# TensorE's order in two stages of a two-block transformer kernel: steps tied to the order in which the program records them

## The chip, the cores and the metric

One core of a Trainium2 chip runs the whole program. The metric is the device time of one execution in microseconds (µs). The engines are TensorE (PE, matrix products; its weight loads are shown as PEld), VectorE (DVE), ScalarE (ACT), GpSimd (POOL) and SyncE (SP), whose queue issues the transfers. Each engine takes the instructions of its own queue in the order that was fixed when the program was compiled.

## What is computed

The reference is two transformer blocks over 1024 tokens of width 1024, in float32. Block 1 projects the normalized input to seven parts and mixes them in two ways. The parts q, f and i feed HGRN, a linear recurrence with a gate per channel, over 4 heads of width 128:

```python
S_new = jnp.exp(b_last[:, :, 0, :])[..., None] * S + jnp.einsum(
    'bhsk,bhsv->bhkv', kb * jnp.exp(b_last - b), vb)
return S_new, o_inter + o_intra
```

The parts sq, sk and sv feed stick-breaking attention, strictly causal, over 8 heads of width 64:

```python
rem = lax.cumsum(log_1mb, axis=3, reverse=True) - log_1mb
a = jnp.where(causal, jnp.exp(jax.nn.log_sigmoid(z) + rem), 0.0)
outs.append(jnp.einsum('bhts,bshd->bthd', a.astype(v.dtype), vp))
```

Both results are normalized (the HGRN one is also gated by hg), joined and multiplied by w_out. A gated feed-forward and an embedding gate follow, and then block 2, with two other kinds of attention, a feed-forward with a convolution, and a gate.

## The kernel before, in words

Every projection is done in three matmuls (mm3, lines 300 to 302): weights and activations are split into a high and a low part, and high by high, high by low and low by high are added in one PSUM bank. A weight unit is 128 x 1024 numbers. Its life is: a load (line 110) into one of two raw buffers; a cast to the high part on ScalarE (line 218); a subtraction for the low part on VectorE or GpSimd (line 224); its matmuls; then its buffer, one of four, is free for the next unit. All transfers are issued from SyncE's queue.

**Steps.** The two stages in question are written as lists of steps. A step is a pair of a cost in assumed µs and a function that records the step's instructions on all engines. A projection step is six matmuls of 512 columns (a_steps and b_steps: a group of 24 matmuls in four steps of 5.1 / 4 = 1.275 each); the fourth step of a group also records what empties the bank, and lets the next weight units be split (pump).

**HGRN stage** (mix1, hgrn_steps). Head 0's own projections (16 steps) and the first two HGRN steps of head 0 are recorded one after the other (run). Then merge interleaves two lists. The first holds the other HGRN steps. Each head has 12: diag (cost 1.7; line 732), seven levels for n = 1, 2, 4, ... 64 (1.7 each; line 746), kt (0.9; transposes, line 779), ds (1.7; line 796) and two outputs (1.7 each; lines 818 and 820). A level multiplies the running q and k products on TensorE, then VectorE multiplies half of q (line 763) and GpSimd half of k (line 764) by the products of gates, and the next level needs both. The second list holds 112 projection steps: head 1's q and f, the first half of pair 0 for the other attention, head 2's q and f, the second half of pair 0, head 3's q and f, sv in 32 steps, and pair 1.

**Stick-breaking stage** (sb, attention_steps, pv_steps). The first list has 236 attention steps with a sum of costs of 119.28, the second the 64 projection steps that mix1 returns (pairs 2 and 3, and the gate hg), with a sum of 81.6. For a head and a block of 128 rows, score multiplies q by k (lines 968, 969; line 971 adds the mask), ScalarE takes two sigmoids (lines 972, 973), VectorE runs a scan along the row (line 975) and a product (line 977). For two blocks of rows and two of columns, one step transposes (line 869), ScalarE and VectorE split the result (lines 872, 873), and a later step multiplies it by the values (lines 882, 886, 888) in the stage's one bank for values; when a pair of row blocks is through, ScalarE copies half of that bank (line 892) and VectorE adds it up (line 983). After two heads, after_pair transposes the pair's result (line 992), takes squares (line 996) and stores it (line 999). Transposes have two banks, scores three, projections two; the split operand has two buffers.

**What sets the order.** merge takes from its first list while that list's share of its cost is at most by times the share of the second list. That is the order in which instructions are recorded. The compiled order is another thing: the tile framework's scheduler goes through the program with its own timing, and gives each engine, whenever it is free, the ready instruction with the lowest priority number. The number is the place of recording; around a step of the first list, merge lowers it by ahead, which is 0 for the HGRN stage and 300 for the stick-breaking stage (AHEAD). So where a step is not ready in the scheduler's timing, the engine's queue gets a later one first.

**After the two stages** out1 multiplies the two results by w_out: for each 128 tokens, prep loads the HGRN output, its gate and the attention output and transposes the gated HGRN output (line 288); mm does two groups of matmuls for each half of the columns, the first on the HGRN part, the second on the attention part. Its weight units take the buffers that the hg units leave.

Of the kernel before, what the change touches and what calls it, by code (L numbers as in the profile page):

```python
# [43 lines left out]
AHEAD = dict(hg=0, sb=300, mla=-20, diff=100)  # L44
BY = dict(hg=1.05, sb=1.0, mla=0.75, diff=1.0)
# [151 lines left out]
class Kernel:  # L197
# [125 lines left out]
        self.u = [self.up.tile([P, 2, 8, 512], F32R, tag="u", name=f"u{h}") for h in range(2)]  # L323


    def merge(self, main, side, ahead=0, by=1.0):


        tc = self.tc
        tm, tsd = sum(c[0] for c in main) or 1, sum(c[0] for c in side) or 1  # L330
        i = j = 0
        a = b = 0.0
        while i < len(main) or j < len(side):
            one = j >= len(side) or (i < len(main) and a / tm <= by * b / tsd and (len(main[i]) < 3 or j >= main[i][2]))
            f = (main[i] if one else side[j])[1]
            if one:
                a, i = a + main[i][0], i + 1
                tc.cur_priority -= ahead
                f()
                tc.cur_priority += ahead  # L340
            else:
                b, j = b + side[j][0], j + 1
                f()


    def a_units(self, name, c0, n):
# [296 lines left out]
    def mix1(self):  # L643
        nc, S, U = self.nc, self.S, self.U
        st = nc.sync.dma_start
        with ExitStack() as c:
            vp = self.pool("hg_v", 1, ctx=c)
            tmp = self.htmp = self.tmp
            v = vp.tile([P, NT, 512], F32, name="hg_vt")
            self.hg_v = v  # L650
            self.first(v)
            self.constants_late()
            self.hp = self.pool("hg", 2, ctx=c)
            self.h1p = self.pool("hg1", 1, ctx=c)
            H = [dict() for _ in range(4)]

            def ev_q(h):
                def f(ps, half):
                    if half == 0:
                        H[h]["q"] = self.hp.tile([P, T], F32, tag="q", name="hq")  # L660
                    s = tmp.tile([P, 512], F32, tag="s", name="sg")
                    nc.scalar.activation(s, ps, AF.Sigmoid)
                    nc.vector.tensor_tensor(H[h]["q"][:, half * 512:(half + 1) * 512], ps, s, ALU.mult)
                return f

            def ev_f(h):
                def f(ps, half):
                    if half == 0:
                        H[h]["f"] = self.hp.tile([P, T], F32, tag="f", name="hf", bufs=1)
                        H[h]["k"] = self.hp.tile([P, T], F32, tag="k", name="hk")  # L670
                    c = slice(half * 512, (half + 1) * 512)
                    lb, mlb = self.lb[:, 0, h:h + 1], self.lb[:, 1, h:h + 1]
                    s = tmp.tile([P, 512], F32, tag="s", name="sg")
                    nc.scalar.activation(s, ps, AF.Sigmoid)
                    nc.vector.tensor_scalar(H[h]["f"][:, c], s, mlb, lb, op0=ALU.mult, op1=ALU.add)
                    s = tmp.tile([P, 512], F32, tag="s", name="sg")
                    nc.scalar.activation(s, ps, AF.Sigmoid, scale=-1.0)
                    nc.vector.tensor_scalar(H[h]["k"][:, c], s, mlb, None, op0=ALU.mult)
                return f

            def ev_T(dst, j):
                def f(ps, half):
                    t = tmp.tile([P, 2, 512], F32R, tag="hl", name="stage")
                    self.split(t[:, 0, :], t[:, 1, :], ps, "act", "dve")
                    c = slice(half * 512, (half + 1) * 512)
                    for e in range(2):
                        st(out=dst[2 * j + e, :, c].rearrange("(a r) t -> r a t", a=2), in_=t[e * 64:(e + 1) * 64].bitcast(F32))
                return f

            def ev_sv(ps, i):  # L690
                t = tmp.tile([P, 8, 2, 64], F32R, tag="hl", name="stage")
                self.split(t[:, :, 0, :], t[:, :, 1, :], ps.rearrange("p (h d) -> p h d", h=8), "act", "dve")
                st(out=S["sv"][i * P:(i + 1) * P], in_=t.rearrange("p h a d -> p h (a d)").bitcast(F32))

            def ev_gate(ps, i):
                s = tmp.tile([P, 512], F32, tag="s", name="sg")
                nc.scalar.activation(s, ps, AF.Sigmoid)
                nc.vector.tensor_tensor(s, ps, s, ALU.mult)
                st(out=S["hgg"][i * P:(i + 1) * P, :], in_=s)

            def head(h):
                return self.a_steps(U["hq", h][0], ev_q(h)) + self.a_steps(U["hf", h][0], ev_f(h))

            def pair(j):
                return (self.a_steps(U["sq", j][0], ev_T(S["sq"], j))
                        + self.a_steps(U["sk", j][0], ev_T(S["sk"], j)))

            first = head(0)
            p0 = pair(0)
            main = head(1) + p0[:8] + head(2) + p0[8:] + head(3) + self.b_steps(U["sv"], self.u_of, ev_sv) + pair(1)  # L710
            side = []
            for h in range(4):
                side += self.hgrn_steps(h, H[h])
            self.run(first + side[0:2])
            self.merge(side[2:], main, AHEAD["hg"], BY["hg"])
        return pair(2) + pair(3) + self.b_steps(U["hg"], self.u_of, ev_gate)

    def hgrn_steps(self, h, X):
# [220 lines left out]
    def sb(self, rest):  # L939
        nc, S, U, A = self.nc, self.S, self.U, self.A  # L940
        self.banks = {"d": [0, 1], "z": [2, 3, 4], "tr": [5, 6], "pv": [7]}
        with ExitStack() as c:
# [56 lines left out]
                nc.sync.dma_start(out=S["osbT"][j * P:(j + 1) * P, :], in_=o)  # L999

            side = self.attention_steps(8, load, score, make_put, after_pair, ORDER["sb"], lambda h: max(0, h // 2 - 1) * 16)
            self.merge(side, rest, AHEAD["sb"], BY["sb"])


    def out1(self):
# [4 lines left out]
        with ExitStack() as c:  # L1010
# [15 lines left out]
            def prep(i):  # L1026
                o = ip.tile([P, 512], F32, tag="o", name="o_hg")
                ld(out=o, in_=S["ohg"][i * P:(i + 1) * P, :])
                gt = ip.tile([P, 512], F32, tag="gt", name="gate")
                ld(out=gt, in_=S["hgg"][i * P:(i + 1) * P, :])  # L1030
                sb = ip.tile([P, 4, P], F32, tag="sb", name="o_sb")
                ld(out=sb, in_=S["osbT"][:, i * P:(i + 1) * P].rearrange("(k p) t -> p k t", p=P))
                r = self.rstd_sqrt(self.square_sum(o, 512), 512)
                nc.gpsimd.tensor_tensor(gt, o, gt, ALU.mult)
                nc.vector.scalar_tensor_tensor(out=o, in0=gt, scalar=r, in1=g_hg, op0=ALU.mult, op1=ALU.mult)
                OT[i] = u = op.tile([P, 2, 8, P], F32R, tag="oT", name="oT")
                self.split(u[:, 0, 4:8, :], u[:, 1, 4:8, :], sb, "act", "gps")
                return lambda: self.transpose_split(o, u, 0, 0, 4)
# [937 lines left out]
```

## Time and profile before

| | |
|---|---|
| Median of 3 executions | 2896.67 µs (2895.93 to 2899.95) |
| The profiled execution | 2897.28 µs, span 2895.5 µs |
| TensorE busy, share of the span | 2777.6 µs, 96% |
| VectorE busy | 1756.3 µs, 61% |
| ScalarE busy | 1163.4 µs, 40% |
| GpSimd busy | 712.3 µs, 25% |
| Mean granted TensorE clock | 0.991 of full speed |

The span runs from the first instruction's start to the last one's end; the execution's time has 1.8 µs more around it. Times of rows are µs from the span's start. In the rows, PE is TensorE, SPq the queue of SyncE; "bank" is a PSUM bank, hk and hg_qp are the running k and q products of HGRN, be and om the rows of the attention, at the transposed ones. Matmuls are pipelined and their ends are modelled, so the durations of neighbours overlap: what a matmul costs is the time from its start to the next one's. Idle time in brackets is that of the engine just before the row, with what ended it.

### The profile page before, as it was taken

To read this page: it belongs to the slowest core of one execution; us is meant where nothing else is said; L and a number is where in the kernel's file an instruction comes from. 1 tells how busy PE (TensorE), PEld (TensorE's weight loads), DVE (VectorE), ACT (ScalarE), POOL (GpSimd) and SP (SyncE) were. 2 spreads that over 40 slices of the span, in tenths; PEclk is the share of its full clock that TensorE was granted. 3 is DMA by queue.
4 is the path that set the end of the run, shared out by engine and by line. 5 is a ranking of instruction groups with operands and counts; after the bars stand their busy time and mean duration, and the time that the engine had idled before them with its cause. 6 is when DMAs were issued, how large, how long until landed. Compare 5 with 4: busy or idle time off the path is not lost. (4 is left out here: it accounts for less than half of the span.)

```text
span 2895.5 us, 37271 instructions
## 1 busy us (share of the span) xinstructions
PE 2777.6 (96%) x13699; PEld 2281.7 (79%) x13699; DVE 1756.3 (61%) x3132; ACT 1163.4 (40%) x2237; POOL 712.3 (25%) x608
## 2 busy tenths in 40 slices
PE   8989998988999999999999999989999999999999
PEld 6878767776888888887788788767778888788887
DVE  4444598768444334667478775777875555556661
ACT  4211376745333334223246455656543333311131
POOL 1222100035433332223124000020243343222211
PEclk9989999999999999999999999999999999999999
DMA  4221645252322224332126855753422222343211
GB/s 134 73 71 65 175 124 135 93 183 73 95 87 84 83 78 165 102 104 91 65 102 178 217 151 175 203 131 76 139 73 81 80 88 87 118 166 104 77 65 46
DMA packets 277942, 321.36 MB, mean 111 GB/s; under 512 B 14646, under 2 KB 207194, under 8 KB 276222
## 3 DMA queue, kind: packets, MB, share of 16 engines
q1 hardware_dynamic: 277758, 318.97, 36.5%
q8 instruction: 108, 1.77, 0.3%
q14 instruction: 76, 0.62, 0.1%
HBM read 228.69 MB, written 92.59 MB: 111 GB/s over the span
## 5 line engine op out<-in xcount | busy, mean ns | idle before, releaser
L1249 PE MATMUL bank<-q,w 128*128 128x512 f32 x3696 | 846.6, 391 | 5.9 <-DVE q L1132 1.4
L1249 PEld LDWEIGHTS bank<-q,w 128*128 128x128 f32 x3696 | 693.3, 188 | 157.6 <-ACT s L1186 2.1
L218 ACT CAST w<-raw 128x1024 fp32r<-128x1024 f32 (+2 forms) x246 | 236.8, 971 | 495.9 <-DVE y L1315 185.9
L224 DVE TENSOR_TENSOR w<-raw,w 128x1024 fp32r<-128x1024 f32 (+2 forms) x242 | 311.7, 1297 | 128.1 <-ACT w L218 121.7
L1315 DVE TENSOR_TENSOR y<-y,bank 128x512 f32<-128x512 f32 x336 | 227.0, 686 | 162.1 <-PE bank L302 158.3
L300 PE MATMUL bank<-w,act 128*128 128x512 f32 x704 | 274.7, 390 | 2.7 <-DVE o L1231 2.7
L302 PE MATMUL bank<-w,act 128*128 128x512 f32 x704 | 274.7, 391 | 1.5 <-POOL act L224 1.5
L300 PE MATMUL bank<-w,u 128*128 128x512 f32 (+1 forms) x672 | 272.0, 405 | 3.1 <-DVE dn L1574 1.4
L301 PE MATMUL bank<-w,act 128*128 128x512 f32 x704 | 274.5, 390 | 0.0
L301 PE MATMUL bank<-w,u 128*128 128x512 f32 (+1 forms) x672 | 266.4, 396 | 3.3 <-POOL w L224 2.2
L302 PE MATMUL bank<-w,u 128*128 128x512 f32 (+1 forms) x672 | 265.9, 396 | 1.1 <-DVE u L296 1.1
L224 POOL TENSOR_TENSOR act<-act_raw,act 128x1024 fp32r<-128x1024 f32 x40 | 103.6, 2609 | 300.9 <-ACT act L218 300.9
L1186 ACT COPY s<-bank 128x512 f32<-128x512 f32 x132 | 77.4, 588 | 202.6 <-PE bank L1249 202.5
L300 PEld LDWEIGHTS bank<-w,act 128*128 128x128 f32 x704 | 132.6, 188 | 30.7 <-DVE o L1231 3.1
L302 PEld LDWEIGHTS bank<-w,act 128*128 128x128 f32 x704 | 132.5, 188 | 30.0 <-POOL act L224 2.2
L301 PEld LDWEIGHTS bank<-w,act 128*128 128x128 f32 x704 | 132.4, 188 | 27.2
L300 PEld LDWEIGHTS bank<-w,u 128*128 128x128 f32 x672 | 127.3, 189 | 26.6 <-ACT u L293 2.4
L301 PEld LDWEIGHTS bank<-w,u 128*128 128x128 f32 x672 | 127.2, 189 | 26.8 <-POOL w L224 3.1
L302 PEld LDWEIGHTS bank<-w,u 128*128 128x128 f32 x672 | 127.0, 189 | 26.2 <-DVE u L296 1.7
L224 DVE TENSOR_TENSOR w<-s,w 128x1024 fp32r<-128x1024 f32 x44 | 54.4, 1236 | 139.9 <-ACT w L218 139.9
L873 DVE TENSOR_TENSOR at<-bank,at 128x512 fp32r<-128x512 f32 (+1 forms) x160 | 99.8, 630 | 42.8 <-ACT at L872 41.6
L140 POOL TENSOR_TENSOR s<-raw 128x512 f32<-128x512 f32 x44 | 59.9, 1362 | 218.3 <-DVE w L224 137.4
(361 smaller groups left out, 5208.9 us busy)
## 6 DMA issues: line engine op xcount, KB each, us to landing
raw<-in_w_gate_up_dram SPq DMA_DIRECT2D x44, 512.0 KB
act<-o SPq DMA_DIRECT2D x88, 256.0 KB
raw<-in_w_down_dram SPq DMA_DIRECT2D x44, 512.0 KB
act_raw<-act SPq DMA_DIRECT2D x44, 512.0 KB
raw<-in_w_in_dram SPq DMA_DIRECT2D x40, 512.0 KB
qk<-qkT SPq DMA_DIRECT2D x32, 384.0 KB
raw<-in_w_gate_dram SPq DMA_DIRECT2D x22, 512.0 KB
raw<-in_w_up_dram SPq DMA_DIRECT2D x22, 512.0 KB
```

The costliest lines, as they stand in the source:

```text
L140: pool(x[:, HI], r2[:, LO], r2[:, HI], ALU.add)
L218: nc.scalar.copy(hi, src)
L224: e.tensor_tensor(lo, src, hi.bitcast(F32), ALU.subtract)
L300: mm(ps, lh, rh, start=start, stop=False)
L301: mm(ps, lh, rl, start=False, stop=False)
L302: mm(ps, ll, rh, start=False, stop=stop)
L873: nc.vector.tensor_tensor(at[:, 1, 0:w], ps[:, 0:w], at[:, 0, 0:w].bitcast(F32), ALU.subtract)
L1186: nc.scalar.copy(t, src)
L1249: nc.tensor.matmul(ps, w[:, a, o], (uh, ul)[b][:, k, :], start=bool(first) and n_mm == 0, stop=n_mm == 11, skip_group_check=True)
L1315: nc.vector.tensor_tensor(y, y, ps, ALU.add)
```

## The change

merge gets a parameter, fixed. With it, each step is recorded inside tc.issue_after(last), where last is the TensorE instruction that was recorded last before the step. This call of the tile framework gives every instruction that the step records on TensorE an edge to last: it is placed behind it in TensorE's queue, and does not wait for its end. So no TensorE instruction of a step can be placed ahead of the step before it. Other engines get no edge, and neither do instructions outside the two calls. The HGRN and the stick-breaking stage use it; two other calls of merge stay as they are.

```diff
-    def merge(self, main, side, ahead=0, by=1.0):
+    def merge(self, main, side, ahead=0, by=1.0, fixed=False):
         tc = self.tc
+        traced = self.nc.cur_bb.bb.instructions
+
+        def step(f):
+            last = next((x for x in reversed(traced) if x.engine == self.nc.tensor.engine), None) if fixed else None
+            with tc.issue_after(last) if last is not None else ExitStack():
+                f()
+
...
                 a, i = a + main[i][0], i + 1
                 tc.cur_priority -= ahead
-                f()
+                step(f)
                 tc.cur_priority += ahead
             else:
                 b, j = b + side[j][0], j + 1
-                f()
+                step(f)
...
-            self.merge(side[2:], main, AHEAD["hg"], BY["hg"])
+            self.merge(side[2:], main, AHEAD["hg"], BY["hg"], fixed=True)
...
-            self.merge(side, rest, AHEAD["sb"], BY["sb"])
+            self.merge(side, rest, AHEAD["sb"], BY["sb"], fixed=True)
```

## Rows read from the trace of the kernel before

**Rows 1.** The page: busy µs of each engine, share of the span, instructions.

```profile
PE 2777.6 (96%) x13699; PEld 2281.7 (79%) x13699; DVE 1756.3 (61%) x3132; ACT 1163.4 (40%) x2237; POOL 712.3 (25%) x608
```

**Rows 2.** Stretches (µs): length, then busy and count of each engine, PEclk, DMA.

```profile
90.62:113.64 23.02, 21.04 (x129) 17.34 (x128) 13.73 (x15) 2.62 (x4) 9.91 (x11) 1.00 0.30 106
...
163.90:169.90 6.00, 3.51 (x32) 3.40 (x32) 2.16 (x3) 0.00 (x0) 1.09 (x1) 1.00 0.00 0
169.90:187.00 17.10, 10.75 (x61) 10.05 (x60) 4.93 (x10) 4.14 (x6) 5.75 (x3) 0.50 0.00 1
...
338.65:565.18 226.53, 206.20 (x1227) 162.49 (x1226) 199.52 (x259) 152.76 (x379) 5.95 (x60) 1.00 0.43 116
565.18:577.69 12.51, 12.51 (x59) 10.33 (x58) 5.98 (x16) 11.44 (x27) 3.11 (x2) 1.00 0.85 289
577.69:620.00 42.31, 33.60 (x138) 25.79 (x136) 27.42 (x47) 19.35 (x36) 16.37 (x10) 0.93 0.65 213
```

**Rows 3.** TensorE's timeline, head 0's front: start, µs, line, shapes, [idle before].

```profile
91.43 0.48 PE L300 MATMUL bank<-u,w 128*128 128x512 f32 x1
...
96.35 1.99 PE L746 MATMUL bank<-hg_qp,hk 128*127 128x64 f32 x16 [0.34 <-DVE hg_qp L727]
...
99.61 0.40 PE L301 MATMUL bank<-u,w 128*128 128x512 f32 x1
100.65 1.94 PE L746 MATMUL bank<-hg_qp,hk 128*126 128x64 f32 x16 [0.64 <-DVE hg_qp L763]
...
104.75 1.92 PE L746 MATMUL bank<-hg_qp,hk 128*124 128x64 f32 x16 [0.49 <-DVE hg_qp L763]
...
108.66 1.86 PE L746 MATMUL bank<-hg_qp,hk 128*120 128x64 f32 x16 [0.33 <-DVE hg_qp L763]
```

**Rows 4.** TensorE's timeline, three of head 1's steps.

```profile
164.46 1.86 PE L746 MATMUL bank<-hg_qp,hk 128*120 128x64 f32 x16 [0.56 <-DVE hg_qp L763]
168.25 1.76 PE L746 MATMUL bank<-hg_qp,hk 128*112 128x64 f32 x16 [1.93 <-DVE hg_qp L763]
172.32 2.83 PE L746 MATMUL bank<-hg_qp,hk 128*96 128x64 f32 x16 [2.31 <-POOL hk L764]
```

**Rows 5.** ScalarE's timeline around head 1's copies and the two weight casts.

```profile
179.44 0.58 ACT L750 COPY hg_sc<-bank 64x512 f32<-64x512 f32 x1 [32.98 <-PE bank L746]
...
183.64 1.99 ACT L218 CAST w<-raw 128x1024 fp32r<-128x1024 f32 x2
```

**Rows 6.** SyncE's queue: the bias transfer and the weight loads behind it.

```profile
78.96 0.73 SPq L572 DMA_DIRECT2D skew<-bias  x1
82.77 18.24 SPq L110 DMA_DIRECT2D raw<-in_w_in_dram  x2
```

**Rows 7.** VectorE in 340 to 566, by line and shape: count, busy µs, mean ns, idle before.

```profile
L873 DVE TENSOR_TENSOR at<-bank,at 128x512 fp32r<-128x512 f32 x48 | 32.4, 679 | 3.1 <-ACT at L872 2.9
L975 DVE TENSOR_TENSOR_SCAN om<-om,zeros 128x1024 f32<-128x1024 f32 x8 | 18.3, 2282 | 0.5 <-ACT om L972 0.4
...
L983 DVE TENSOR_TENSOR sb_o<-bank,ot 64x256 f32<-64x256 f32 x32 | 13.1, 411 | 2.4 <-ACT ot L892 1.9
...
L977 DVE TENSOR_TENSOR be<-be,om 128x1024 f32<-128x1024 f32 x8 | 9.7, 1215 | 0.1
```

**Rows 8.** ScalarE in 340 to 566, the same view.

```profile
L872 ACT CAST at<-bank 128x512 fp32r<-128x512 f32 x48 | 28.2, 593 | 21.0 <-PE bank L869 20.5
...
L973 ACT ACTIVATE be<-bank 128x512 f32<-128x512 f32 x40 | 24.1, 603 | 0.0
...
L892 ACT COPY ot<-bank 64x256 f32<-64x256 f32 x32 | 11.8, 370 | 9.9 <-PE bank L888 9.4
...
L996 ACT ACTIVATE junk<-bank 128x128 bf16<-128x128 f32 x28 | 8.1, 289 | 1.2 <-PE bank L992 1.0
```

**Rows 9.** TensorE's waits in 338 to 566: total µs, times, longest.

```profile
PE bank L882 <- DVE sb_o L983: 10.0, 16, 1.2
```

**Rows 10.** TensorE's timeline, the first matmul of the output stage.

```profile
580.37 0.50 PE L300 MATMUL bank<-w,oT 128*128 128x512 f32 x1 [2.24 <-ACT oT L293]
```

## The prediction

> **What bounds the kernel now.** The page comes first: TensorE is busy for 96% of the span [rows 1], so time is won or lost only where TensorE waits or runs slowly. The change touches two stages, so the second view is the table of stretches [rows 2]. Read there the share of TensorE and its granted clock. Head 0's front of the HGRN stage (90.62 to 113.64) loses 2.0 µs of idle time. From 163.90 to 187.00, in head 1, TensorE is busy for 14.3 of 23.1 µs, and for 17.1 of them the granted clock is 0.50, which is 1.2 GHz. The stick-breaking stage (338.65 to 565.18) leaves 20.3 µs idle while VectorE is busy for 199.5 of 226.5 µs. Behind it stand 54 projection matmuls alone: 12.5 µs with no idle time, 0.23 µs a matmul, and VectorE is busy there for only 6.0 µs.
>
> The third view is the program's order. In merge the HGRN steps that are left sum to 75.0 (4 heads of 19.6, less two steps of 1.7) and the projection steps to 112 × 1.275 = 142.8. A level of 1.7 is 2.27% of its list, a projection step 0.89%; with by = 1.05 some 2.4 steps of six matmuls, 14 matmuls or 3.3 µs, follow each level. I counted the matmuls of lines 300 to 302 ahead of each HGRN step in the trace against these sums. They agree within two (records can be missing) from level 16 of head 0 to level 4 of head 1 (336 to 474) and from head 2's first step to the end (594 to 918). **They differ in two places**: head 0's front, and head 1 from level 8 to its outputs, which all stand behind 480 matmuls where the program has 486 to 582. Only there does the tie move TensorE in this stage.
>
> **The change, part by part.** It adds no instruction. It takes from the scheduler the choice of what TensorE does next at a step's border; VectorE, ScalarE, GpSimd and the DMA queue are placed anew around that order.
>
> **Head 1 of HGRN: −14.0.** Idle time is 2.49 + 6.35 = 8.84 µs [rows 2]: each level waits for the VectorE or GpSimd product of the level before, with no filler between [rows 4]. The 10.75 busy µs of the slow stretch take 5.4 at 2.4 GHz, so 5.3 more; together 14.2, less some 0.2 for a short wait such as other heads have. The tie puts 12 to 18 matmuls (2.8 to 4.1 µs) between levels. A level needs 4.3 µs from start to start, 2.0 of it TensorE's own (from 96.35 to 100.65 in [rows 3]), so 2.3 µs of cover are enough.
>
> Why there was no filler matters, since the tie could put TensorE before the same obstacle. The next projection step was that of head 2's forget gate. Its two weight casts ran on ScalarE at 183.64, after ScalarE had idled for 33 µs, and behind head 1's copies in its queue [rows 5]; their loads had been issued by 101 [rows 6]. So the place in the queue was late, not the data. A 2.4 MB bias transfer was issued just ahead of those loads, at 78.96 [rows 6]; I read the order as one made by a scheduler that expected them late. Under the tie the cast must stand ahead of head 1's level 8 on ScalarE, or the program could not end, and there it finds an idle engine. What stays is its VectorE half (1.2 µs), likely placed behind level 4's products: **+1.0**, bounded by 0 and by 3 (a sigmoid, the cast and the VectorE half one after the other, 0.6 + 1.05 + 1.2).
>
> **Head 0's front: +3.8.** The first two steps are recorded before the merge, and every projection step of the merge stands behind level 2. The 20 matmuls that now fill the gaps up to 100.65 (from 91.43 to 99.61, 20 of them) [rows 3] move behind it: 20 × 0.23 = 4.6 µs. Level 2 comes no earlier, since each step there already ended a wait for VectorE. Behind it the program has 18 and 12 matmuls where the trace has 7 and 7, so the waits of 0.49 and 0.33 at 104.75 and 108.66 go: 4.6 − 0.8 = 3.8.
>
> **The clock at that front: +1.0**, between 0 and 5. The row nearest to it is head 1's, where gaps of 0.56 and 1.93 µs preceded the fall to 0.50 [rows 2, 4]; the new front has gaps of about 1.8, 1.8 and 2.3 in 10 µs, but then 18 matmuls without one. If the fall comes, two levels cost 1 µs more each, and a part of the 18 matmuls (4.1 µs) doubles. I take 1.0 as the middle of no fall and a short one.
>
> The Trainium skill (TensorE: Matmul & The Clock Gate, "HAM oscillation — how this bites in real kernels") says that waits between groups of matmuls throw the clock back to its lower level, so that the work behind starts slowly; by that rule this term would be an estimated 4 to 5 µs and the total some 3 to 4 µs longer. The trace agrees where gaps come in a row (0.50 from 169.9 to 187.0), and disagrees for single ones: the stick-breaking stage keeps 1.00 with 20 µs of gaps.
>
> **The stick-breaking stage and its hand-over: −3.0.** Gains and losses nearly balance here. Now attention steps are pulled ahead by a priority of 300, and the projections lag until 54 are left over (12.5 µs). Tied, 64 projection steps lie evenly between 236 attention steps, so these 54 become filler. But TensorE can no longer go round a wait. To size the new waits I walked all steps in the program's order with start-to-start intervals of this trace (transposes 0.109, 256-column matmuls 0.118, 512-column ones 0.235 µs), each other engine taking what is ready, attention first. TensorE's work is 195.6 µs: 90.2 of projections, 31.4 of transposes, 34.1 of values, 36.4 of scores, 3.5 at the pairs' ends. The waits sum to 42.2:
> - transposes behind the rows they need, 14.8: sigmoid 0.60, scan 2.28, product 1.22 [rows 7, 8] are 4.1 µs, against some 3 µs of steps between; 7.7 of the 14.8 fall on head 0, where no older work is queued;
> - values behind their split operand, 11.7: 0.59 + 0.68 µs, plus a scan that happens to be running;
> - values behind the add that frees the only bank, 10.4: 0.37 + 0.41 and three hops make 0.9; today's idle from this cause is 10.0 [rows 9];
> - steps behind the four squares of a bank at a pair's end, 5.3 [rows 8].
>
> 195.6 + 42.2 = 238. The same walk over today's order, taken from the trace, ends at 244.7 where the trace has 241.1 (the last gate's product): it runs 1.5% long. Other choices of VectorE's and ScalarE's order moved the tied walk between 237 and 246. On the trace's scale, projections end some 6 µs earlier than 577.69, but attention ends some 8 µs later than 565.4. The output stage needs both: its weights follow the projections' end, its second operand the last pair's store. Today its first group starts at 580.37 after 2.24 idle [rows 10] and its second half near 583. Tied, the first half can start near 576 and the second near 580. That is −3.0, bounded by −9 (all waits behind 580 vanish as well) and by +9 (the walk's upper end, and nothing won at the hand-over).
>
> **Sum:** −14.0 + 1.0 + 3.8 + 1.0 − 3.0 = −11.2. The profiled execution took 2897.28 µs (span 2895.5 and 1.8 around it), 0.6 above the median of 2896.67. 2897.3 − 11.2 = 2886.1: I forecast **2886**.
>
> **The rivals.**
> *Late weights take the gain back.* If the cast of head 2's gate still stands behind something late on ScalarE or VectorE, TensorE stops at that step rather than in the levels, and the queue of head 1 stops behind it. For it: two casts, a sigmoid and a store all stood late together. Against: in the tied order little is left that the cast can stand behind, and ScalarE idled for 33 µs [rows 5]. Price: 8 to 12 of the 14 µs come back; 2896.
>
> *The tied attention waits more than the walk says: slower.* VectorE is 88% busy in that stage [rows 2], and each of the 80 transposed groups makes a round trip through ScalarE and VectorE to which TensorE is now tied. The walk has 42.2 / 80 = 0.53 µs of wait a group. At 0.75, a quarter of a mean scan more, the stage loses 18: 2904. It decides from 0.14 µs a group (11.2 / 80) on. For it: the order's spacing counts steps by assumed costs, not by VectorE's time. Against: the walk stayed below 246 for every order of the other engines.
>
> *The tie does nothing*, as priorities give the order anyway: so it is for most of three HGRN heads, but not in the stretches that carry the sum.
>
> **How the numbers follow.** Forecast 0.62, late weights 0.20, tied waits 0.15, no effect 0.03. A measurement of this kernel can tell about 0.2%, 5.8 µs, from no change. Faster is the forecast's 0.62, same the 0.23 of late weights and no effect, slower 0.15. The forecast alone reaches from 2874 (no half clock, −9 at the attention) to 2891; late weights carry the range to 2897, and the lower part of the slower case to 2901.
>
> **What would show it.** After the change head 1's levels should stand 12 to 18 matmuls apart with the clock at 1.00; the two casts should run on ScalarE before head 1's level 8; head 0's first four HGRN steps should stand with no projection between; no run of 54 projections should follow the attention; TensorE's idle time should rise in the attention, mostly ahead of lines 869 and 882, to about 40 µs. It is wrong if idle time there passes 55 µs, or if TensorE waits over 5 µs at head 2's gate.

## The result and the profile after

The changed kernel takes **2925.9 µs** (median) against 2896.3 for the kernel before in the same comparison: a ratio of 1.0105, 95% interval 1.0093 to 1.0117. It is slower by some 30 µs where 11 µs less were forecast, and outside the range. The profiled execution has a span of 2924.3, 28.8 more than before.

Where the 28.8 went, by the start or end of the same instructions in the two traces:

| from, to | before | after | difference | predicted |
|---|---|---|---|---|
| head 0's first scores to head 1's (HGRN) | 55.1 | 63.4 | +8.3 | +4.8 |
| head 1 to head 2 | 70.1 | 58.3 | −11.8 | −13 |
| head 2 to the first score of the attention | 124.8 | 125.6 | +0.8 | 0 |
| first score to the end of attention and projections | 237.1 | 265.5 | **+28.3** | with the next row, −3 |
| to the first matmul of the stage behind the output stage (line 1126, now 1134) | 47.9 | 53.2 | **+5.3** | |
| from there to the end of the span | 2269.9 | 2267.8 | −2.1 | 0 |

The HGRN stage did what was forecast, with a dearer front: the first score stands at 337.93 instead of 340.57. The stick-breaking stage and its hand-over lost 33.6.

The table of stretches of the kernel after, in the columns that [rows 2] have (length; busy µs of each engine with counts; granted clock of TensorE; share of the DMA engines; GB/s):

```profile
90.72:115.00 24.28, 18.50 (x90) 16.53 (x89) 10.87 (x12) 2.02 (x3) 8.76 (x10) 0.72 0.29 102
...
154.07:212.34 58.27, 56.38 (x343) 48.60 (x342) 29.92 (x38) 13.63 (x20) 12.55 (x14) 1.00 0.30 85
336.10:603.20 267.10, 224.38 (x1279) 181.85 (x1277) 207.70 (x266) 159.94 (x387) 5.95 (x60) 0.96 0.39 106
603.20:614.13 10.93, 0.19 (x3) 0.03 (x1) 5.28 (x16) 8.06 (x23) 1.26 (x1) 0.56 0.94 311
95.92:109.57 13.65, 10.85 (x41) 9.93 (x42) 5.12 (x6) 0.00 (x0) 4.08 (x6) 0.50 0.32 112
409.94:416.77 6.83, 5.57 (x19) 4.50 (x18) 1.25 (x2) 2.70 (x10) 0.00 (x0) 0.50 0.16 65
604.50:624.98 20.48, 7.90 (x22) 6.14 (x23) 11.05 (x24) 10.80 (x28) 6.25 (x5) 0.50 0.90 305
```

Head 1 now runs at clock 1.00 with 1.9 µs of idle time. Head 0's front fell to 0.50 for 13.65 µs. The attention stage is 267.1 long with 42.7 idle; before, its two stretches in [rows 2] were 239.0 with 20.3 idle. Of the stage's 28.1, 22.4 are therefore idle time. The clock makes most of the rest: 409.94 is one of five stretches at 0.50, 20.5 µs together, in which TensorE is busy for 19.2; half of that, 9.6, is what the lower level costs. The two sum to 32.0, 3.9 more than the stage lost. In the walk's counting that remainder is waiting which the modelled ends show as busy: of the 239.0 before, 195.6 are the walk's work and 20.3 idle, which leaves 23.1; the same difference after, 267.1 − 195.6 − 42.7 − 9.6, is 19.2.

TensorE's waits of the kernel after from 336 to 604 (engine and line, releaser, total µs, times, longest), which answer to [rows 9]:

```profile
PE bank L890 <- DVE sb_o L991: 12.3, 16, 1.3
PE bank L877 <- ACT junk L1004: 10.2, 6, 2.1
PE bank L877 <- DVE be L985: 9.3, 13, 2.0
PE bank L890 <- DVE at L881: 8.8, 11, 1.5
```

All line numbers of the two stages stand 8 higher than before: 890 is the values' matmul, 877 the transposes, 991 the add that frees the bank, 1004 the squares at a pair's end. The second line is new; the third was 2.0 before and the fourth 5.0.

How such a wait arises is seen at the first pair's end, in TensorE's and then ScalarE's timeline of the kernel after (start, µs, operation; idle time and releaser in brackets):

```profile
406.41 1.04 PE L1000 MATMUL bank<-ident,sb_o 128*128 128x128 f32 x8
409.57 0.58 PE L877 MATMUL bank<-ident,be 128*128 128x128 f32 x3 [2.12 <-ACT junk L1004]
411.40 1.12 PE L877 MATMUL bank<-ident,be 128*128 128x128 f32 x4 [1.26 <-ACT junk L1004]
```

```profile
407.72 1.14 ACT L1006 ACTIVATE sb_o<-sb_o,cols 128x1024 f32<-128x1024 f32 x1
...
411.16 0.19 ACT L1004 ACTIVATION_READ_ACCUMULATOR junk<-bank 128x1 f32 x1
```

The eight transposes of line 1000 fill both banks that the transposed groups use. ScalarE empties them with eight squares, and has put the scaling of the pair's tile (1.14 µs) among them. The next transposed groups wait 2.12 and 1.26 µs, with projections and scores behind them that could have run, and the clock falls at 409.94, between the two.

VectorE's queue has a part in the other waits. Its timeline, and the values' matmul that waited:

```profile
394.88 0.69 DVE L983 TENSOR_TENSOR_SCAN om<-om,zeros 128x256 f32<-128x256 f32 x1 [0.86 <-ACT om L980]
395.68 0.43 DVE L985 TENSOR_TENSOR be<-be,om 128x256 f32<-128x256 f32 x1
396.14 0.42 DVE L991 TENSOR_TENSOR sb_o<-bank,ot 64x256 f32<-64x256 f32 x1
```

```profile
396.61 0.50 PE L890 MATMUL bank<-at,vs 128*128 128x256 f32 x2 [1.32 <-DVE sb_o L991]
```

The add that frees the bank takes 0.42. Its operand is copied by ScalarE until 395.52, but the product of the next rows goes first, and the add starts at 396.14. That is common: by the instruction just ahead of the releaser on VectorE, 18 of the 21 µs behind lines 881 and 991 end with a split or an add that stood queued behind a scan, a product or another split. How much of each wait the queue makes, and how much the chain itself, isn't shown by this.

Last, the hand-over in TensorE's timeline:

```profile
602.95 0.44 PE L1000 MATMUL bank<-ident,sb_o 128*128 128x128 f32 x2 [0.60 <-DVE sb_o L991]
614.13 1.09 PE L288 MATMUL bank<-ident,o_hg 128*128 128x128 f32 x4 [10.74 <-DVE rs_h L258]
```

No projection is left behind the last pair. The output stage's first operand is loaded by a transfer that SyncE issues at 604.97, just behind the pair's store; its norm is done at 613.98 (line 1043; the row names the VectorE instruction behind it). TensorE stands for 10.74 µs and then works at clock 0.50 up to 624.98.

### The profile page after: what moved, and what is told of

The parts are those of the page before. It is cut to its first block, busy times and chain, and to the rows that moved or that the text cites. A ratio compares the mean times of both kernels' runs of the same rounds, so it can differ in the third digit from the quotient of the medians.

```text
span 2924.3 us, 37258 instructions
## 1 busy us (share of the span) xinstructions
PE 2781.7 (95%) x13699; PEld 2292.4 (78%) x13699; DVE 1762.3 (60%) x3132; ACT 1163.1 (40%) x2235; POOL 703.2 (24%) x608
## 5 line engine op out<-in xcount | busy, mean ns | idle before, releaser
L224 DVE TENSOR_TENSOR w<-raw,w 128x1024 fp32r<-128x1024 f32 (+2 forms) x242 | 314.3, 1307 | 126.7 <-ACT w L218 125.6
L301 PE MATMUL bank<-w,u 128*128 128x512 f32 (+1 forms) x672 | 267.1, 397 | 2.8 <-POOL w L224 1.6
L881 DVE TENSOR_TENSOR at<-bank,at 128x512 fp32r<-128x512 f32 (+1 forms) x160 | 100.2, 630 | 47.9 <-ACT at L880 46.9
```

Source lines behind the costliest of these rows:

```text
L224: e.tensor_tensor(lo, src, hi.bitcast(F32), ALU.subtract)
L301: mm(ps, lh, rl, start=False, stop=False)
L881: nc.vector.tensor_tensor(at[:, 1, 0:w], ps[:, 0:w], at[:, 0, 0:w].bitcast(F32), ALU.subtract)
```

## The experiments

Every ratio is against the kernel before, run beside it on the same chip. The experiments stand on four chips, on which the kernel before has medians of 2895.9 to 2896.7, and a profiled execution lies up to 6.5 µs off its kernel's median; so differences of a few µs between two experiments say little.

**The two ties apart.** First the HGRN tie alone:

```diff
-            self.merge(side, rest, AHEAD["sb"], BY["sb"], fixed=True)
+            self.merge(side, rest, AHEAD["sb"], BY["sb"])
```

> The tie in the HGRN stage alone; the stick-breaking stage is as before. Theory A (the two ties add up: the HGRN tie gained 2.6 us up to the first score, the other one lost the rest): the first score stands near 338, attention and hand-over take what they took before, about 2893.5 (2.5 to 3 below before). Rival B (the HGRN tie hands on a worse start, so that a part of the loss seen behind 338 comes from it): the stage behind 338 is over 5 us longer than before, 2900 or more.

Measured 0.9983 (0.9974 to 0.9992), 2891.4 against 2896.0; first score at 337.13, and the attention takes what it took (224.9 µs from the first score to the last step, against 224.6). Then the other tie alone:

```diff
-            self.merge(side[2:], main, AHEAD["hg"], BY["hg"], fixed=True)
+            self.merge(side[2:], main, AHEAD["hg"], BY["hg"])
```

> The tie in the stick-breaking stage alone. Theory A: all of the loss is here: 2896 + 32 = 2928 (from 2926 to 2931); TensorE's idle time in the stage about 43 us as with both ties, against 20 before, the output stage's first transposes 10 us or more behind the last attention step. Rival B: under 2920.

1.0135 (1.012 to 1.0151), 38 µs by the medians; the profiled execution is 31 longer (span 2926.8). Idle time from the first score to the last attention step 41.4, and 10.9 at the hand-over. The whole loss is the stick-breaking tie's; rival B falls.

**Where the HGRN tie gains and loses.** The tie begins behind the tenth projection step, which is head 0's level 32. From level 16 of head 0 to level 4 of head 1 the trace had the program's order anyway, so in effect the tie begins at head 1:

```diff
-    def merge(self, main, side, ahead=0, by=1.0, fixed=False):
+    def merge(self, main, side, ahead=0, by=1.0, fixed=False, since=0):
...
-            last = next((x for x in reversed(traced) if x.engine == self.nc.tensor.engine), None) if fixed else None
+            last = next((x for x in reversed(traced) if x.engine == self.nc.tensor.engine), None) if fixed and j >= since else None
...
-            self.merge(side[2:], main, AHEAD["hg"], BY["hg"], fixed=True)
+            self.merge(side[2:], main, AHEAD["hg"], BY["hg"], fixed=True, since=10)
...
-            self.merge(side, rest, AHEAD["sb"], BY["sb"], fixed=True)
+            self.merge(side, rest, AHEAD["sb"], BY["sb"])
```

> The HGRN tie begins at head 1's first step; head 0 and the stick-breaking stage are as before. Theory A (head 1's 4 gaps and its half clock are won, the loss of 8.4 us at head 0's front is the tie's own, 5 of it a half clock): head 2 begins near 204, against 215.8 before, first score near 329, total 2884.5 (10 to 13 below before). Rival (head 1's gain needs the front's order, since the casts of head 2's weights move ahead only with it): head 1 keeps gaps of over 4 us, total 2890 or more.

0.9967 (0.9955 to 0.998), 2886.3. Its table of stretches, head 0, head 1 and the attention:

```profile
90.45:145.47 55.02, 53.06 (x326) 44.99 (x325) 23.68 (x34) 8.82 (x15) 18.67 (x21) 1.00 0.19 61
145.47:203.63 58.16, 56.42 (x344) 48.59 (x343) 29.95 (x38) 13.62 (x20) 12.40 (x14) 1.00 0.31 84
328.73:553.62 224.89, 204.09 (x1219) 160.92 (x1217) 198.94 (x258) 151.20 (x376) 5.95 (x60) 1.00 0.43 115
```

Head 1 gains its 12 µs without the front, and the attention takes what it took; the hand-over takes some 2 µs more. Second, the tie from the start, with head 0's first two steps inside the merge so that projections lie between them:

```diff
-            self.run(first + side[0:2])
-            self.merge(side[2:], main, AHEAD["hg"], BY["hg"], fixed=True)
+            self.run(first)
+            self.merge(side, main, AHEAD["hg"], BY["hg"], fixed=True)
...
-            self.merge(side, rest, AHEAD["sb"], BY["sb"], fixed=True)
+            self.merge(side, rest, AHEAD["sb"], BY["sb"])
```

> The HGRN tie from the start, but head 0's first two steps stand inside the merge, so that projections are spread from the first step on; the stick-breaking stage untied. Theory A (the front lost 8.4 us in the tied order because the program had no projections there, and the half clock came of those gaps): no half clock ahead of head 1, head 1 begins within 2 us of 145.5, total that of the tie from head 1 on, 0.9967 of before (2886). Rival (the tie itself costs at the front, whatever the program's order): head 1 begins at 150 or later, 2890 or more.

0.9958 (0.9944 to 0.9971), 2885.1. Of its timeline the front, and of its table of stretches the front and head 1:

```profile
93.07 1.16 PE L740 MATMUL bank<-hq,hk 128*128 128x128 f32 x8 [1.78 <-DVE hk L686]
...
98.19 1.88 PE L754 MATMUL bank<-hg_qp,hk 128*127 128x64 f32 x16
...
102.72 1.54 PE L754 MATMUL bank<-hg_qp,hk 128*126 128x64 f32 x13
```

```profile
90.23:115.00 24.77, 22.99 (x142) 20.26 (x141) 12.76 (x15) 3.22 (x5) 8.80 (x10) 1.00 0.30 105
...
148.35:209.31 60.96, 57.96 (x344) 49.91 (x342) 28.22 (x38) 11.97 (x18) 13.99 (x14) 0.97 0.34 96
```

In the front one gap of 1.78 is left, and the clock stays at 1.00. Head 1 begins at 148.35, later than I expected, but with 450 projection matmuls ahead of it in the trace instead of 432 (18 × 0.23 = 4.1 µs). Head 1 takes 60.96, 2.8 more than with the front untied: TensorE waits 2.67 µs there for the late weights of head 2's gate (1.14 in the changed kernel), and the clock is at 0.50 for 3.4 µs. The first score stands at 329.21, against 328.73. So the front's loss came from the program's order there, not from the tie as such.

**Three causes inside the stick-breaking tie, one at a time.** Two banks for the values, two for the scores (HGRN untied in this and the next two):

```diff
-        self.banks = {"d": [0, 1], "z": [2, 3, 4], "tr": [5, 6], "pv": [7]}
+        self.banks = {"d": [0, 1], "z": [2, 3], "tr": [5, 6], "pv": [7, 4]}
```

> As the run with the stick-breaking tie alone, but with two banks for the values and two for the scores (instead of one and three). If the wait for the add that frees the only bank of values (12.3 us of idle time in the changed kernel) is a cost of its own: that wait falls under 2 us and the total falls by 8 to 14 below the run with that tie alone, near 2918. Rival (TensorE then waits for VectorE at the next transposed group or split instead, as the round trips pace it): idle time moves to those waits, total within 4 us of the run with that tie alone.

1.0085 (1.007 to 1.01), 2919.9, 13.6 less than the tie alone. The wait for the add is gone; that for the split grew from 8.9 to 13.2, as the rival has it:

```profile
PE bank L890 <- DVE at L881: 13.2, 16, 2.0
...
PE bank L877 <- ACT junk L1004: 10.2, 6, 2.1
PE bank L877 <- DVE be L985: 7.2, 11, 1.8
```

Both are true in part; idle time fell by 8.2 (41.4 to 33.2). Next, the pair's end in the scores' banks:

```diff
             def after_pair(j, X):
                 o = X[2 * j]["o"]
                 for g in range(2):
-                    ps = self.ps("tr")
+                    ps = self.ps("z")
```

> The stick-breaking tie alone, and the eight transposes at a pair's end take their banks from the scores' three instead of the two that the transposed groups use. The run with that tie alone was 1.0135 of before (2896). Theory A (at a pair's end the next two transposed groups wait in the tied order until four squares have emptied a bank: 10.1 us of idle time, and a half clock of 3.4 to 6.8 us behind each of three pairs, which costs half of that): this wait falls under 1 us, and the slow stretches behind the pairs go; 10 + 7 = 12 to 17 us less, 1.0085 of before (2920). Rival (the scores wait for the squares in their place, since TensorE can still not go round): idle time moves to the scores' line, total within 5 us of the tie alone.

1.0075 (1.0061 to 1.0088), 2918.2, by the medians 15 less than the tie alone.

```profile
PE bank L890 <- DVE sb_o L991: 10.9, 14, 1.3
PE bank L877 <- DVE be L985: 9.1, 13, 2.0
PE bank L890 <- DVE at L881: 8.9, 11, 1.5
PE bank L976 <- ACT be L981: 1.8, 3, 0.6
```

The 10.1 for the squares is gone, 1.8 came up at the scores, and no stretch at 0.50 begins behind one of the three pairs' ends inside the stage any more. This one was its own cause. Half clock is not gone, though: five stretches elsewhere in the stage make 17.1 µs, against 23.9 with the tie alone. Third, the projections lag:

```diff
-            self.merge(side, rest, AHEAD["sb"], BY["sb"], fixed=True)
+            self.merge(side, rest, AHEAD["sb"], 1.17, fixed=True)
```

> The stick-breaking tie alone, with the attention ahead of the projections by 1.17, so that about 54 projection matmuls are left behind the last attention step, as before the change. Theory A (10.9 us of wait and 20 us of half clock at the hand-over come from attention and projections ending together): the wait ahead of the output stage falls under 3 us and the half clock there to 3 to 7 us, 8 + 7 = 15 us less; the attention pays with 54 x 0.23 = 12.5 us less cover, of which I take a half: total 6 to 12 us below the tie alone, 2921 to 2925. Rival (the hand-over is what the output stage's weights and norms cost in any order): the wait ahead of the output stage stays over 8 us and the total is that of the tie alone or more.

1.0099 (1.0085 to 1.0113), 2925.7, by the medians 8 less than the tie alone. The 54 projections stand behind the attention (591.14 to 603.90, no idle time), and the output stage starts without a wait; but its second and a later group wait for the norm:

```profile
PE bank L288 <- DVE o_hg L1043: 7.3, 2, 4.0
```

So the hand-over is paid in part in any order: in the traces the stage is 5.1 µs shorter than with the tie alone (projections included) and the way from there to line 1134 only 2.9, where I had expected most of the gain. By the profiled executions the three mends take 11, 10 and 6 µs off the tie alone, by the medians 14, 15 and 8.

**The same mends where TensorE is free to go round.** With the HGRN tie from head 1 on and the stick-breaking stage untied: two banks for the values; the pair's end in the scores' banks; and two banks with the pair's end in them.

> The HGRN tie from head 1 on, the stick-breaking stage untied, with two banks for the values and two for the scores. The same without the banks was 0.9967 of before (2886). If the 10.0 us that TensorE idles for the add that frees the only bank are its own: attention ends 5 to 9 us earlier, but 54 projections stand behind it, so the total gains what becomes of the sum of both, 4 to 8 us: 2880. Rival (the free order already goes round what matters, and two banks for scores make them wait): within 3 us of 2886 either way.

> The HGRN tie from head 1 on, the stick-breaking stage untied, the transposes at a pair's end in the scores' banks. In the free order no wait for the squares stands in the trace of before: theory A says 2886 within 2 us, and with that that the pair ends are a cost of the tied order alone. Rival: the free order hides a cost of the pair ends in other waits; 2882 or less.

> The HGRN tie from head 1 on, the stick-breaking stage untied, two banks for the values, and the pair's end in these banks. Each alone was 0.995 of before. If both gains are there and separate: 0.9935 (2878). Rival (each was the hand-over's chance, not the banks): 0.995 to 0.997.

0.9951 (0.9938 to 0.9963), 0.9946 (0.9932 to 0.9959) and 0.9955 (0.9942 to 0.9969); without a mend 0.9967. The intervals overlap, and the first two medians (2882.6 and 2882.2) fall between what I had named for either side; the third is the rival's. The attention's length barely moves (224.9 without, 223.5, 223.7 and 225.5 with). Most of the 4 to 5 µs that the first two medians gain lies between its last step and line 1134's first matmul (62.8 without, 58.3 and 58.8 with), and the run with the HGRN tie alone has 58.4 there with no mend at all. So I read it as the hand-over's chance: a gain from the banks is shown for the tied order only.

**All three mends together under the tie**, with HGRN tied from head 1 on; the edits shown above, but the pair's end in the two banks of the values:

```diff
-        self.banks = {"d": [0, 1], "z": [2, 3, 4], "tr": [5, 6], "pv": [7]}
+        self.banks = {"d": [0, 1], "z": [2, 3], "tr": [5, 6], "pv": [7, 4]}
...
-                    ps = self.ps("tr")
+                    ps = self.ps("pv")
...
-            self.merge(side, rest, AHEAD["sb"], BY["sb"], fixed=True)
+            self.merge(side, rest, AHEAD["sb"], 1.17, fixed=True)
```

> The HGRN tie from head 1 on, and the stick-breaking tie with all three mends: two banks for the values, the pair's end in these banks, a lag of 1.17. Theory A (the causes are separate, the mends of 12, 13 and 8 us add up against the 33 to 37 us of the tie): 2886 + 35 - 33 = 2888, 0.997 of before, from 2884 to 2893. Rival (the mends share the same waits, which VectorE's round trips set): TensorE's idle time in the stage stays over 30 us, total 2897 or more.

1.0004 (0.9995 to 1.0013), 2897.3: the sum (2888) did not come, the total is the rival's (2897 or more), and the idle time just under its 30. The attention takes 233.3 where the untied one takes 224.9, and idles for 28.9 against 20.8. The tie costs 11 µs by the medians even so, some 8 of them in the attention; what is left are waits for VectorE:

```profile
PE bank L890 <- DVE at L881: 15.8, 13, 3.4
PE bank L877 <- DVE be L985: 8.8, 11, 1.9
```

**What is left.** Values one group later, with a third buffer for the split operand, in this stage only, under the tie alone:

```diff
-    def attention_steps(self, heads, load, score, make_put, after_pair, order, need=lambda h: 0):
+    def attention_steps(self, heads, load, score, make_put, after_pair, order, need=lambda h: 0, GL=GL):
...
-            self.atp = self.pool("at", ATB, ctx=c)
+            self.atp = self.pool("at", ATB + 1, ctx=c)
...
-            side = self.attention_steps(8, load, score, make_put, after_pair, ORDER["sb"], lambda h: max(0, h // 2 - 1) * 16)
+            side = self.attention_steps(8, load, score, make_put, after_pair, ORDER["sb"], lambda h: max(0, h // 2 - 1) * 16, GL=2)
```

> The stick-breaking tie alone, with each group's values one group further behind its transposes, and a third buffer for the split operand. Theory A (8.9 us of the idle time are the round trip of a split, which the tied order leaves too little time): that wait falls under 3 us, 4 to 8 us less than the tie alone (1.0135), 1.011 of before. Rival (VectorE's own queue is late, the wait moves to the next use): total within 3 us of the tie alone.

1.011 (1.0096 to 1.0124). The wait for the split vanished and the one for the add grew from 11.9 to 31.3, as the rival has it:

```profile
PE bank L890 <- DVE sb_o L991: 31.3, 16, 3.3
```

From first score to the attention's last step it takes 265.4, as the tie alone (265.3). By the medians it is some 5 faster, with intervals that touch; the profile shows no gain. Then the products behind the scans on GpSimd, first under the tie alone, then untied:

```diff
-                nc.vector.tensor_tensor(be[:, 0:ext], be[:, 0:ext], om[:, 1:ext + 1], ALU.mult)
+                nc.gpsimd.tensor_tensor(be[:, 0:ext], be[:, 0:ext], om[:, 1:ext + 1], ALU.mult)
```

> The stick-breaking tie alone, with the 64 products behind the scans on GpSimd, which has 6 us of work in that stage, instead of VectorE (48 us of work fewer there; one product of 1024 columns takes about 2.6 us by the GpSimd rows of the same shape instead of 1.2). Theory A (VectorE's queue: in the tied order 7 to 9 us of idle time stand behind a product, 8 more behind a scan): TensorE's waits for VectorE's split and add fall from 21 to under 12 us, the wait for rows rises by less; 1.009 of before or less (the tie alone: 1.0135). Rival (the length of the chain scan, product, transposes): waits for rows rise by more than 10 us, 1.013 or more.

> The HGRN tie from head 1 on, the stick-breaking stage untied, the 64 products on GpSimd. Theory A (VectorE, 88% busy, sets the free order's 20 us of idle time too): idle time in the stage falls under 14 us, total 2878 to 2883, 0.994 of before. Rival (the longer chain of a row costs more than the queue's relief): idle time 20 us or more, 2886 or more.

1.0128 (1.011 to 1.0147), and untied 0.9988 (0.9979 to 0.9996), 6 worse than the same without. Under the tie:

```profile
PE bank L877 <- POOL be L985: 18.0, 17, 2.6
PE bank L890 <- DVE at L881: 11.4, 12, 1.6
...
PE bank L890 <- DVE sb_o L991: 4.2, 6, 0.7
```

The waits for split and add fell from 20.8 to 15.6 (under 12 were expected), those for rows rose from 9.1 to 18.0. Both numbers of the rival nearly came out (1.0128 for 1.013, a rise of 8.9 for 10), but its reason isn't shown by them: VectorE's scans grew longer too (last section), so the relief was partly taken back. Untied, the attention takes 231.7 with 25.6 idle, instead of 224.9 with 20.8, as the rival there has it. Whether queue or chain weighs more in the last 8 µs stays open.

**The fastest versions** are those with the HGRN tie mended, the stick-breaking tie left out and the products on VectorE: 0.9946 to 0.9967, 2882 to 2886.

## Why the prediction was wrong

**The step that failed** is the attention's walk, which gave the tied order too little waiting: "The waits sum to 42.2" and "195.6 + 42.2 = 238". In the walk's own counting a matmul ends where the next begins. So counted, the stage had 239.0 − 195.6 = 43.4 µs of waits before and has 71.5 after: 9.6 are the half clock, and some 62 are waits, where the walk has 42.2. Where it went wrong is known in part. It let VectorE and ScalarE take what served the attention, while in the tied kernel most splits and adds that TensorE waited for stood queued behind other work; how much of the 20 that makes stays open. One of its terms was plainly too small: for the steps behind the squares at a pair's end it has 5.3, and the trace 10.2 of idle time alone, with the scaling of the pair's tile and a split among ScalarE's squares. And it held the clock at full.

One addition would have warned me. The profile counts a matmul as busy to its modelled end: 218.7 µs of busy time for the same stage before. I named "idle time … to about 40" as a sign, in the profile's counting; 42.7 were measured. But 218.7 busy and 40 idle are 259 and not 238: the sign spoke against my own sum.

**The hand-over** was booked as a gain because both streams end together. Nothing is then left to cover the norm's load and its chain: +5.3 instead of part of −3. The row that spoke for it was there: 12.5 µs of projections with no idle time [rows 2] ahead of 2.24 idle [rows 10] hid what stands behind the pair's store.

**The rival "the tied attention waits more"** (0.15, 2904) was the right mechanism: 28.3 µs over 80 groups are 0.35 a group (the clock's part included), above the 0.14 from which it decides, and the hand-over came on top. Its argument against, that the walk stayed below 246 for every order, was the walk speaking for itself.

**HGRN.** Head 1: −13 forecast, −11.8 measured. The casts moved as said: two stand on ScalarE at 154.75, before any level, where [rows 5] had them at 183.64, and the wait for head 2's gate is 1.14, so "late weights" fell. ScalarE's row and TensorE's:

```profile
154.75 2.00 ACT L218 CAST w<-raw 128x1024 fp32r<-128x1024 f32 x2
```

```profile
173.88 0.50 PE L302 MATMUL bank<-u,w 128*128 128x512 f32 x1 [1.14 <-DVE w L224]
```

The front's filler (+3.8) measured 8.3 − 5.4 = 2.9. Its clock was mis-sized: +1.0 forecast, 10.85 / 2 = 5.4 measured. TensorE's timeline there:

```profile
93.55 1.16 PE L740 MATMUL bank<-hq,hk 128*128 128x128 f32 x8 [1.78 <-DVE hk L686]
96.44 3.68 PE L754 MATMUL bank<-hg_qp,hk 128*127 128x64 f32 x16 [1.73 <-DVE hg_qp L735]
102.39 3.64 PE L754 MATMUL bank<-hg_qp,hk 128*126 128x64 f32 x16 [2.27 <-DVE hg_qp L771]
```

The clock fell at 95.92, behind the gap of 1.78 and within that of 1.73; the third gap was part of the slow stretch. And each of the two levels took 3.7 µs instead of 2.0 ([rows 3]), 1.7 more where I had said 1.

The rule of the Trainium skill (TensorE: Matmul & The Clock Gate, "HAM oscillation — how this bites in real kernels"), that waits between groups of matmuls throw the clock back, was taken to give 4 to 5 for that term, and this trace agrees with that (5.4), though the waits in that section's own example are longer than the front's gaps.

My reading against it was that the attention before kept 1.00 through 20.3 µs of gaps, so that only gaps in a row count. The front's gaps do stand in a row, and I had taken a fifth of the price all the same. The tied attention refutes the reading itself: at 362.16 its clock fell behind a single gap of 1.84, longer than any in the attention before (1.5). But the length of one gap doesn't decide it either: a gap of 2.04 at 345.98 left the clock at 1.00, and at 560.13 it fell behind gaps of 1.24 and 0.40.

```profile
345.98 0.55 PE L877 MATMUL bank<-ident,be 128*128 128x128 f32 x3 [2.04 <-DVE be L985]
...
362.18 0.90 PE L877 MATMUL bank<-ident,be 128*128 128x128 f32 x3 [1.84 <-DVE be L985]
```

**Signs and range.** The signs that I named came true: levels 12 to 18 matmuls apart, both casts early, no projection in the front (three steps, not four), no run of 54, idle time near 40. None of them measured the stage's length. And the lower end of the range doesn't follow from its terms: with no half clock and −9 at the attention the sum is 2879, not 2874.

## What to carry to other kernels

An engine that may go round a wait hides round trips, shared banks and the end of a stage all at once; before its order is fixed, price each of these as a wait with what is queued behind it. Fix the order where the trace shows the free order failing (head 1), not in a whole stage whose engines answer at uneven times. And test a forecast with busy + idle = length in the profile's own counting.

## What was not expected of the hardware

With the products on GpSimd, VectorE's scans take longer. VectorE's groups of the tie alone, then of the version with the products on GpSimd (mean ns of one, idle before):

```profile
L983 DVE TENSOR_TENSOR_SCAN om<-om,zeros 128x640 f32<-128x640 f32 x8 | 11.9, 1487 | 0.1
...
L983 DVE TENSOR_TENSOR_SCAN om<-om,zeros 128x128 f32<-128x128 f32 x8 | 3.3, 417 | 0.0
```

```profile
L983 DVE TENSOR_TENSOR_SCAN om<-om,zeros 128x640 f32<-128x640 f32 x8 | 15.6, 1952 | 2.2 <-ACT om L980 2.2
...
L983 DVE TENSOR_TENSOR_SCAN om<-om,zeros 128x128 f32<-128x128 f32 x8 | 14.2, 1773 | 0.1
```

A scan of 128 columns takes 1773 ns on average instead of 417. Seven of the eight run beside the product of 1024 columns (2.0 µs) on GpSimd: they start 0.2 to 0.3 µs behind its start and end 0.3 behind its end. The eighth has no product beside it and takes 424. One of the seven, in VectorE's and GpSimd's timelines:

```profile
397.66 1.95 DVE L983 TENSOR_TENSOR_SCAN om<-om,zeros 128x128 f32<-128x128 f32 x1
```

```profile
397.34 2.00 POOL L985 TENSOR_TENSOR be<-be,om 128x1024 f32<-128x1024 f32 x1 [3.17 <-DVE om L983]
```

Scans of 1024 columns have no product beside them there and keep their time (2292 against 2285). The Trainium skill (SBUF — State Buffer, "SBUF: two separate sides") says that a VectorE operation with two inputs in SBUF and a GpSimd operation that reads SBUF share a port pair, which the one that starts first holds for its whole instruction while the other stands still. The trace agrees: the scan has two inputs in SBUF, and ends 0.3 µs behind the product that started before it.
